# Three token-mixing branches emitted in steps between weight pieces, and one broadcast matmul in two float32r parts

## The chip, the cores and the metric

The kernel runs on one core of a Trainium2 chip. The time is device microseconds of one execution; the number compared is the median of several runs, and a profile is one further execution with its own time. The engines are called as the profile calls them: PE (TensorE, with PEld for its weight loads), DVE (VectorE), ACT (ScalarE) and SP, whose queue issues the DMAs.

## The reference, cut to what matters

The network is two blocks on 256 tokens of 2048 channels, all in float32. The second block, which alone is touched, has two layers; each is a mixing stage and a feed-forward stage. A mixing stage projects the normalised input and feeds four branches, whose outputs (512 channels each) are joined by one output matrix:

```python
p = (u @ w_in[l]).astype(jnp.float32)
p_ret, p_hgrn, p_ml, p_rw = split_cols_2(p, GROUP_COLS)
o_ret = retention_group(p_ret)
o_hgrn = hgrn2_group(p_hgrn, lower_bounds[l], hgrn_norm_w[l])
o_ml = mlstm_group(p_ml, ...)
o_rw, v_first = rwkv7_group(p_rw, v_first, ...)
mixed = jnp.concatenate([o_ret, o_hgrn, o_ml, o_rw], axis=-1) @ w_out[l]
h = h + rms_norm_2(mixed, norm_post_mix[l])
```

Each branch has 8 heads of 64 channels and is a linear attention over the tokens with a decay of its own: fixed per head in retention, from a gate per channel in hgrn, from two gates per head in mlstm. In mlstm the scores of a head are `q k^T * exp(log_decay - m_t)`, where `m_t` is a running maximum over the tokens; the output is divided by `max(|sum of scores|, exp(-m_t))`.

## The kernel before

Every large product reads its weights once from memory, in pieces of 128 x 1024 values (512 KB, three buffers). A piece is split by `weights` (L208) into two float32r parts: ACT copies `whi`, DVE subtracts to get `wlo`; `mm3` (L220, its matmuls on L223) then makes three matmuls, high by high, high by low and low by high. In the projections of the mixing stage a piece is 24 matmuls of 256 columns, in the output matrix 12 of 512 columns. `by_channels`, `by_tokens1` and `group_block` walk over the pieces and after each piece call `next(self.side, None)`, which emits one step of a generator; only the rwkv branch is such a generator.

In each mixing stage (`mixing`, L1639) the order of emission is: rwkv's projections; mlstm's gates; mlstm for heads 0 to 3 and for heads 4 to 7 ("halves"); hgrn's first half; the part of the output matrix for mlstm; hgrn's second half; retention's first half; the output part for hgrn; retention's second half; what is left of rwkv; the output parts for rwkv and, last, for retention. Each half is four projections (16 pieces) and then its inner part, emitted in one go.

The inner parts, with the lines that the trace names:

- mlstm: `decays` makes an exponent per head in one PSUM bank: two bf16 matmuls (L1266) put in the causal mask, and L1268 adds the running maxima `MX` of the head to all 128 partitions. L1268 is a float32 matmul with 8 rows and 384 columns, which the trace lists as two records; there are four in a half, 16 in all. ACT takes the exponentials (L1271). Then `pair_scores` (L1092), a product on DVE (L1279), the head's output (`head_out`, L1099 to L1101, 64 columns each) and its denominator (L1283 to L1285, one column each); afterwards a normalisation.
- hgrn: eight levels, each with exponentials, two transposes, four scores (L1178), masks, four outputs (L1188).
- retention: four heads; a table of decays comes by DMA (L1070, issued by SP), the scores are multiplied by it on DVE (L1075), then `head_out`.

The stages' tiles come from pools by tag with a fixed number of buffers (`g2` 12, `a3` 2), and a scheduler orders the instructions of each engine: what was emitted earlier goes first when its inputs are ready by the scheduler's own estimate. The order is fixed in the program, and on the chip each engine keeps to it.

Of the kernel before, what the change touches and what calls it, by code (L numbers as in the profile page):

```python
# [114 lines left out]
SECOND = dict(r2=16, g2=12, r1=5, a3=2, vf=2, mx=1, lora=1, nmu=1, mid=4, st=1, rtab=2, gate=3, den=2)  # L115
# [24 lines left out]
class Emitter:  # L140
    def __init__(self, tc, st, a, gains):
# [6 lines left out]
        self.side = iter(())  # L148
# [76 lines left out]
    def by_tokens(self, xg, w, c0, n):  # L225
# [3 lines left out]
        for k in range(0, 16, j):  # L229
# [6 lines left out]
            next(self.side, None)  # L236
        return [o[:, :n] for o in out]

    def by_channels(self, xg, w, c0, n):
# [5 lines left out]
        for k in range(0, 16, j):  # L245
# [7 lines left out]
            next(self.side, None)  # L253
# [22 lines left out]
    def group_block(self, yg, w, k0, cb):  # L276

        ps = [self.bank("m") for _ in range(2)]
        for k in range(0, 4, 2):
# [5 lines left out]
            next(self.side, None)  # L285
# [733 lines left out]
    def by_tokens1(self, xg, w, c0, n):  # L1019
# [3 lines left out]
        for k in range(0, 16, j):  # L1023
# [7 lines left out]
            next(self.side, None)  # L1031
# [17 lines left out]
    def retention(self, hf, xg, w, rows, tabs, yg):  # L1049
# [15 lines left out]
        o = self.bank("o").rearrange("p (m c) -> p m c", m=2)  # L1065
        for h in range(4):
            if h % 2 == 0:
                dec = self.t([P, 2, T], "g2")
                h0 = 4 * hf + h
                nc.sync.dma_start(dec, self.a["decay"][:, h0 * T : h0 * T + 2 * T].rearrange("p (h t) -> p h t", h=2))  # L1070
            if h % 2 == 0:
                pss = self.pair_scores(qT, kT, h // 2)
            ps = pss[h % 2]
            a = self.t([P, 384], "a3")
            nc.vector.tensor_mul(a[:, :T], ps[:, :T], dec[:, h % 2])  # L1075
            nc.vector.tensor_mul(a[:, T:], ps[:, T : T + P], dec[:, h % 2, :P])
            self.head_out(o, a, h, v)
        of = o.rearrange("p m c -> p (m c)")
        f = self.head_scale(of, 8, 64)
        y = self.t([P, 512], "y")  # L1080
        y3 = y.rearrange("p (h d) -> p h d", h=8)
        nc.vector.tensor_mul(y3, of.rearrange("p (h d) -> p h d", h=8), f.unsqueeze(2).to_broadcast([P, 8, 64]))
        nc.vector.tensor_mul(y, y, sz.rearrange("p m c -> p (m c)"))
        self.turned_rows(lambda b: self.split([q[:, 2 * hf : 2 * hf + 2] for q in yg], b), y)
# [18 lines left out]
    def hgrn(self, l, hf, xg, w, yg):  # L1103
# [38 lines left out]
        dg = g2()  # L1142
        nc.vector.tensor_mul(dg, q, k)
        nc.vector.tensor_mul(dg, self.pair_sums(dg, 2)[0], v)
        o = self.bank("o").rearrange("p (a t) -> p a t", a=2)
        nc.tensor.matmul(o.rearrange("p a t -> p (a t)"), self.c("ident"), dg.rearrange("p a t -> p (a t)"),
                         start=True, stop=False, skip_group_check=True)
        for h in (128, 64, 32, 16, 8, 4, 2, 1):
            nb = T // (2 * h)
            cm = cum[128 if h >= 32 else 32]  # L1150

            hv = lambda x, i: x.rearrange("p a (b j k) -> p (a b) j k", j=2, k=h)[:, :, i]
            cp = lambda x: x.rearrange("p a (b k) -> p (a b) k", k=h)
            n = 2 * nb
            ex = self.t([P, 2, 2, P], "g2")
            eq, ek = ex[:, 0], ex[:, 1]
            mid = hv(cm, 0)[:, :, h - 1 : h].to_broadcast([P, n, h])
            if h == 128:
                nc.vector.tensor_copy(cp(eq), hv(cm, 1))
            else:  # L1160
                nc.vector.tensor_sub(cp(eq), hv(cm, 1), mid)
            nc.vector.tensor_sub(cp(ek), mid, hv(cm, 0))
            nc.scalar.activation(ex, ex, AF.Exp)
            nc.vector.tensor_mul(cp(eq), cp(eq), hv(q, 1))
            nc.vector.tensor_mul(cp(ek), cp(ek), hv(k, 0))

            vh = self.t([P, 384], "a3")[:, :T].rearrange("p (a c) -> p a c", a=2)
            nc.scalar.copy(cp(vh), hv(v, 0))
            b = self.bank()[:, :T].rearrange("p (a c) -> p a c", a=2)
            self.transposes([b[:, i] for i in range(2)], [vh[:, i] for i in range(2)])  # L1170
            vc = self.t([P, 384], "a3")[:, :T]
            nc.scalar.copy(vc, b.rearrange("p a c -> p (a c)"))
            am = self.t([P, 2, 2, P], "g2")
            pss = [self.bank()[:, :T].rearrange("p (a t) -> p a t", a=2) for _ in range(2)]
            for i in range(2):
                for par in range(2):
                    r = slice(64 * par, 64 * par + 64)
                    nc.tensor.matmul(pss[par][:, i], ek[r, i], eq[r, i], start=True, stop=True)  # L1178
            for par in range(2):
                if h == 128:  # L1180
                    nc.scalar.copy(am[:, par], pss[par])
                else:
                    nc.vector.tensor_mul(am[:, par], pss[par], self.c({1: "ident", 64: "pair"}.get(h, f"same{h}")).unsqueeze(1).to_broadcast([P, 2, P]))
# [455 lines left out]
    def mixing(self, l, X):  # L1639
# [20 lines left out]
        for hf in range(2):  # L1660
            self.mlstm(l, hf, xg, w, rows, gates, ys[2])
# [176 lines left out]
```

## Time and profile before

| | us |
|---|---|
| median of 3 runs (lowest, highest) | 3941.05 (3933.78, 3945.38) |
| profiled execution, its own time | 3934.05 |
| its span in the trace | 3932.2 |
| PE busy (matmuls) | 3843.8, 98% |
| DVE busy, ACT busy | 2376.1 (60%), 1806.8 (46%) |
| mean granted clock of PE | 0.983 |

Busy time of PE is that of pipelined matmuls, so a PE that is busy all the time may still work slowly. The granted clock tells how fast: 1.00 stands for 2.4 GHz, 0.50 for 1.2 GHz. The mixing stage of the first layer runs from about 1046 to 1704 us of the span, that of the second from about 2466 to 3170 us; each is followed by a feed-forward stage.

### The profile page before, as it was taken

How to read it: one execution, taken by the hardware profiler on the slowest of the kernel's cores; microseconds unless marked ns; L12 is line 12 of the kernel's file. 1: busy time of each engine (PE TensorE's matmuls, PEld its weight loads, DVE VectorE, ACT ScalarE, POOL GpSimd, SP SyncE). 2: the span in 40 equal slices, each digit the busy share in tenths (PEclk: the TensorE clock that was granted, in tenths of full speed). 3: DMA queues.
4: the chain of work that ended last, by engine and by line, in shares of the span. 5: the costliest groups of instructions: out<-in, count | busy, mean ns of one | idle time of the engine just before them, and what ended most of it. 6: DMA issues, size and time to landing. Idle time of an engine off the chain costs nothing.

```text
span 3932.2 us, 54691 instructions
## 1 busy us (share of the span) xinstructions
PE 3843.8 (98%) x21408; PEld 3220.0 (82%) x21408; DVE 2376.1 (60%) x4126; ACT 1806.8 (46%) x2455; POOL 0.2 (0%) x4
## 2 busy tenths in 40 slices
PE   9999999999999999999999999999999999999998
PEld 7878877788889988878888888888888878888886
DVE  6666677666665565664555556764666565555556
ACT  5545455554543554354443434543554354444433
POOL 0000000000000000000000000000000000000000
PEclk9999999999999999999999999998999999999999
DMA  7664544655643333566666666543334656666665
GB/s 237 193 175 129 165 142 144 177 161 166 198 120 108 108 107 116 170 188 187 186 183 187 183 187 192 152 119 97 92 113 123 188 172 187 183 187 185 186 185 166
DMA packets 402644, 633.64 MB, mean 161 GB/s; under 512 B 28081, under 2 KB 164017, under 8 KB 402385
## 3 DMA queue, kind: packets, MB, share of 16 engines
q1 hardware_dynamic: 399744, 624.70, 53.1%
q10 hardware_dynamic: 2640, 5.44, 0.4%
q8 instruction: 168, 2.75, 0.3%
q14 instruction: 92, 0.75, 0.1%
HBM read 623.77 MB, written 6.29 MB: 160 GB/s over the span
## 4 chain that ended last, share of the span: by engine, by line
PE 77%; DVE 5%; ACT 2%; DMA 2%; issue 1%; DVEq 0%; SPq 0%; ACTq 0%
PE b L223 66%; PE b L317 3%; DVE wlo L218 1%; PE b L1492 1%; PE b L1486 1%; ACT whi L217 1%; PE b L1188 1%; PE b L1092 1%; PE b L1178 1%; DMA g<-in_decay_dram 0%; PE b L1465 0%; PE b L471 0%; PE b L1268 0%; PE b L505 0%; DMA wraw<-in_w_ffn_down_dram 0%
## 5 line engine op out<-in xcount | busy, mean ns | idle before, releaser
L218 DVE TENSOR_TENSOR wlo<-wraw,whi 128x1024 fp32r<-128x1024 f32 x1144 | 1392.5, 1218 | 1080.7 <-ACT whi L217 1078.1
L217 ACT CAST whi<-wraw 128x1024 fp32r<-128x1024 f32 x1144 | 1195.9, 1046 | 1579.6 <-PE b L223 1462.2
L223 PE MATMUL b<-whi,xt 128*128 128x512 f32 (+1 forms) x5888 | 1694.3, 370 | 0.5 <-ACT g L1060 0.5
L223 PEld LDWEIGHTS b<-whi,xt 128*128 128x128 f32 x5888 | 1056.7, 189 | 194.2 <-issue 2.2
L223 PE MATMUL b<-wlo,xt 128*128 128x512 f32 (+1 forms) x2944 | 1083.2, 368 | 3.3 <-DVE wlo L218 3.1
L223 PE MATMUL b<-whi,yt 128*128 128x512 f32 x2304 | 745.1, 400 | 1.5 <-ACT yt L307 1.5
L223 PEld LDWEIGHTS b<-wlo,xt 128*128 128x128 f32 x2944 | 555.3, 189 | 101.9 <-DVE wlo L218 7.6
L223 PEld LDWEIGHTS b<-whi,yt 128*128 128x128 f32 x2304 | 432.6, 188 | 105.2 <-ACT yt L307 2.0
L223 PE MATMUL b<-xt,whi 128*128 128x256 f32 (+3 forms) x2688 | 516.5, 290 | 2.3 <-ACT xt L310 2.0
L223 PE MATMUL b<-wlo,yt 128*128 128x512 f32 x1152 | 459.0, 399 | 0.0
L223 PEld LDWEIGHTS b<-xt,whi 128*128 128x128 f32 (+3 forms) x2688 | 418.4, 189 | 19.2 <-issue 9.3
L223 PE MATMUL b<-xt,wlo 128*128 128x256 f32 (+3 forms) x1344 | 386.0, 287 | 0.0
L223 PEld LDWEIGHTS b<-wlo,yt 128*128 128x128 f32 x1152 | 217.2, 189 | 50.7 <-issue 0.6
L223 PEld LDWEIGHTS b<-xt,wlo 128*128 128x128 f32 (+3 forms) x1344 | 254.0, 189 | 3.9 <-issue 2.1
L223 PE MATMUL b<-whi,g 128*128 128x512 f32 (+1 forms) x384 | 108.1, 361 | 0.4 <-ACT g L307 0.4
L296 DVE TENSOR_TENSOR r<-b,r 128x512 f32<-128x512 f32 x144 | 92.2, 682 | 0.0
L223 PEld LDWEIGHTS b<-whi,g 128*128 128x128 f32 (+1 forms) x384 | 61.7, 162 | 14.3 <-ACT g L307 0.9
L317 PE MATMUL b<-gains,X 128*128 128x128 f32 x232 | 38.0, 300 | 32.6 <-DVE small L384 15.6
L223 PE MATMUL b<-wlo,g 128*128 128x512 f32 (+1 forms) x192 | 68.8, 358 | 0.0
L296 DVE TENSOR_TENSOR X<-b,X 128x512 f32<-128x512 f32 x96 | 62.7, 684 | 5.4 <-PE b L223 5.4
L317 PEld LDWEIGHTS b<-gains,X 128*128 128x128 f32 x232 | 29.9, 155 | 39.4 <-issue 26.0
L485 ACT ACTIVATE soft<-b,small,esmall 128x256 f32<-128x256 f32 (+1 forms) x88 | 44.9, 517 | 36.2 <-DVE small L482 32.6
(468 smaller groups left out, 2855.8 us busy)
## 6 DMA issues: line engine op xcount, KB each, us to landing
wraw<-in_w_in_dram SPq DMA_DIRECT2D x248, 512.0 KB, 3.7
wraw<-in_w_ffn_gate_dram SPq DMA_DIRECT2D x176, 512.0 KB, 3.7
wraw<-in_w_ffn_up_dram SPq DMA_DIRECT2D x176, 512.0 KB, 3.7
wraw<-in_w_ffn_down_dram SPq DMA_DIRECT2D x176, 512.0 KB, 3.7
wraw<-in_w_out_dram SPq DMA_DIRECT2D x128, 512.0 KB, 3.7
wraw<-in_even_w_in_dram SPq DMA_DIRECT2D x104, 512.0 KB, 3.6
wraw<-in_odd_w_in_dram SPq DMA_DIRECT2D x96, 512.0 KB, 3.7
wraw<-in_mem_w_kv_dram SPq DMA_DIRECT2D x32, 512.0 KB, 3.8
```

The costliest lines, as they stand in the source:

```text
L217: nc.scalar.copy(hi, raw)
L218: nc.vector.tensor_sub(lo, raw, hi.bitcast(FT))
L223: self.nc.tensor.matmul(out, l[x], r[y], start=start and i == 0, stop=stop and i == 2, **kw)
L296: self.nc.vector.tensor_add(dst[cb][m], ps[m], dst[cb][m])
L317: self.nc.tensor.transpose(o, s, self.c("ident")[:n, :n])
L485: nc.scalar.activation(pt[:, i], ps3[:, i], AF.Exp, scale=fs[:, i : i + 1], bias=nb[:, i : i + 1], accum_out=sm[:, i : i + 1])
L1092: self.nc.tensor.matmul(res[par][:, c], kT[r, i, ss], qT[r, i, ts], start=True, stop=True)
L1178: nc.tensor.matmul(pss[par][:, i], ek[r, i], eq[r, i], start=True, stop=True)
L1188: nc.tensor.matmul(out, vc[:, i * P + 64 * par : i * P + 64 * par + 64], am[:, par, i], start=False, stop=h == 1, skip_group_check=True)
L1486: mm(ps[:, i].rearrange("p (b k) -> p b k", k=h), gb[0][:, i], left(inv[:, i]), start=True, stop=True)
L1492: mm(ps[:, i], it[:, i], pl[:, i], start=True, stop=True)
```

## The change

The inner parts of mlstm, hgrn and retention become generators, which the three functions return after their projections. `mixing` puts them in a queue; after each weight piece `step` emits one step of rwkv and one step of the first generator in the queue. Before an output part that needs a branch, `end_of` emits what is left of it. A half of mlstm has 7 steps, one of hgrn 10, one of retention 3: 40 in a layer, 80 in all. So a half's inner part stands between the pieces of the next projection or output part. Within mlstm, the exponents of two heads are a step, and each head's product, output and denominator one more.

In `mlstm_gates` the running maxima are split into two float32r parts, by the same ACT copy and DVE subtraction as the weights, and L1268 becomes two float32r matmuls (L1298 of the changed kernel) that add both parts. What is computed stays the same.

```diff
+    def step(self):
+        next(self.side, None)
+        while self.queue:
+            try:
+                next(self.queue[0])
+                return
+            except StopIteration:
+                self.queue.pop(0)
+
+    def end_of(self, gen):
+        while any(q is gen for q in self.queue):
...
-            next(self.side, None)
+            self.step()
...
-        MX = self.t([P, 384], "mx")[:8]
-        nc.vector.tensor_tensor_scan(MX[:, :T], ai, ai, 0.0, OP.max, OP.max)
-        nc.vector.tensor_copy(MX[:, T:], MX[:, P:T])
-        nc.vector.tensor_add(x, F, MX[:, :T])
+        nc.vector.tensor_tensor_scan(M, ai, ai, 0.0, OP.max, OP.max)
+        MX = [self.t([P, 384], "mx", FR)[:8] for _ in range(2)]
+        for c, t in ((slice(0, T), slice(0, T)), (slice(T, 384), slice(P, T))):
+            self.split([q[:, c] for q in MX], M[:, t])
+        nc.vector.tensor_add(x, F, M)
...
-            sel = self.c("ident")[:8, hh : hh + 1].to_broadcast([8, P])
+                sel = self.identr[:, hh : hh + 1].to_broadcast([8, P])
...
-            nc.tensor.matmul(pd[:, :384], sel, MX, start=False, stop=True, skip_group_check=True)
+                for i, q in enumerate(MX):
+                    nc.tensor.matmul(pd[:, :384], sel, q, start=False, stop=i == 1, skip_group_check=True)
...
                     dms = [decays(h + x) for x in range(2)]
+                    yield
                     pss = self.pair_scores(qT, kT, h // 2)
...
                 nc.vector.tensor_copy(den[:, :, h], db)
+                yield
...
-        for hf in range(2):
-            self.mlstm(l, hf, xg, w, rows, gates, ys[2])
-        self.hgrn(l, 0, xg, w, ys[1])
+        ml = [queued(self.mlstm(l, hf, xg, w, rows, gates, ys[2])) for hf in range(2)]
+        hg = [queued(self.hgrn(l, 0, xg, w, ys[1]))]
...
+        self.end_of(ml[1])
         self.out_group(ys[2], wo, 2 * 512, acc, True)
-        self.hgrn(l, 1, xg, w, ys[1])
-        self.retention(0, xg, w, rows, tabs, ys[0])
+        hg.append(queued(self.hgrn(l, 1, xg, w, ys[1])))
+        rt = [queued(self.retention(0, xg, w, rows, tabs, ys[0]))]
+        self.end_of(hg[1])
         self.out_group(ys[1], wo, 512, acc, False)
-        self.retention(1, xg, w, rows, tabs, ys[0])
+        rt.append(queued(self.retention(1, xg, w, rows, tabs, ys[0])))
         for _ in self.side:
             pass
         self.out_group(ys[3], wo, 3 * 512, acc, False)
+        self.end_of(rt[1])
```

What this does to the order on PE is shown at three places. In the changed kernel the lines are shifted: L240 is L223 of before, L1114 is L1092, L1121 to L1123 are L1099 to L1101, L1295 and L1298 are L1266 and L1268, L1314 to L1316 are L1283 to L1285, L1088 is L1070. Names: `b` is a PSUM bank, `xt` the input, `whi` and `wlo` a weight piece, `g` queries, keys and values, `a` the decays times scores.

First place, PE, first half of mlstm in the first layer: from the scores of two heads to the second head's output, before the change.

```order
L1092 MATMUL b_11144<-g_10562,g_10733 128x256
L1092 MATMUL b_11144<-g_10562,g_10733 128x128
L223 MATMUL b_11200<-xt,whi 128x256 x2
L1099 MATMUL b_11091<-g_10899,a_11133 128x64
L1100 MATMUL b_11091<-g_10899,a_11133 128x64
L1101 MATMUL b_11091<-g_10899,a_11133 128x64
L1283 MATMUL b_11143<-consts_307,a_11133 128x1
L1284 MATMUL b_11143<-consts_307,a_11133 128x1
L1285 MATMUL b_11143<-consts_307,a_11133 128x1
L223 MATMUL b_11200<-xt,wlo 128x256
L1099 MATMUL b_11091<-g_10899,a_11140 128x64
L1100 MATMUL b_11091<-g_10899,a_11140 128x64
```

The same place of the changed kernel, around the first head of a pair; the pieces of L240 go on on both sides.

```order
L240 MATMUL b_11097<-xt,wlo 128x256
L240 MATMUL b_11097<-xt,whi 128x256 x2
L1121 MATMUL b_11144<-g_10905,a_11151 128x64
L1122 MATMUL b_11144<-g_10905,a_11151 128x64
L1123 MATMUL b_11144<-g_10905,a_11151 128x64
L1314 MATMUL b_11208<-consts_307,a_11151 128x1
L1315 MATMUL b_11208<-consts_307,a_11151 128x1
L1316 MATMUL b_11208<-consts_307,a_11151 128x1
L240 MATMUL b_11097<-xt,wlo 128x256
L240 MATMUL b_11097<-xt,whi 128x256 x2
L240 MATMUL b_11097<-xt,wlo 128x256
L240 MATMUL b_11097<-xt,whi 128x256 x2
```

Before, two weight matmuls stand ahead of the first head and one between it and the next. Now 11 weight matmuls precede the first head's six small ones and 13 follow them (the other 12 of each lie outside the rows shown); the next weight piece begins after the second head.

Second place, PE, the exponents of two heads in the same half, before.

```order
L223 MATMUL b_11200<-xt,whi 128x256
L1266 LDWEIGHTS identb_9137
L1266 MATMUL b_11129<-laterb,identb_9137 128x128
L1266 LDWEIGHTS identb_9137
L1266 MATMUL b_11129<-laterb,identb_9137 128x128
L1268 MATMUL b_11129<-mx,gains 128x384
L1266 LDWEIGHTS identb_9137
L1266 MATMUL b_11136<-laterb,identb_9137 128x128
L1266 LDWEIGHTS identb_9137
L1266 MATMUL b_11136<-laterb,identb_9137 128x128
L1268 MATMUL b_11136<-mx,gains 128x384
L223 MATMUL b_11200<-xt,whi 128x256
```

And in the changed kernel.

```order
L1520 MATMUL b_11300<-r_11253,r_11128 128x64 x4
L1295 LDWEIGHTS identb_9137
L1295 MATMUL b_11307<-laterb,identb_9137 128x128
L1295 LDWEIGHTS identb_9137
L1295 MATMUL b_11307<-laterb,identb_9137 128x128
L1298 MATMUL b_11307<-mx,identr 128x384 x2
L1295 LDWEIGHTS identb_9137
L1295 MATMUL b_11315<-laterb,identb_9137 128x128
L1295 LDWEIGHTS identb_9137
L1295 MATMUL b_11315<-laterb,identb_9137 128x128
L1298 MATMUL b_11315<-mx,identr 128x384 x2
L240 MATMUL b_11335<-xt,whi 128x256 x2
```

Each float32 matmul of L1268 has become two matmuls of 384 columns, and a whole weight piece now follows where the scores of L1092 followed one weight matmul.

Third place, SP and PE, the second half of retention in the second layer. SP before:

```order
L216 DMA wraw<-in_w_out_dram 128x2x512 x5
L1070 DMA g_27788<-in_decay_dram 128x512
L1070 DMA g_27808<-in_decay_dram 128x512
L216 DMA wraw<-in_w_out_dram 128x2x512 x3
L1602 DMA y<-in_norm_post_mix_dram 128x512
```

SP in the changed kernel, with the lines shifted as on PE (L233 is L216, L1636 is L1602).

```order
L233 DMA wraw<-in_w_out_dram 128x2x512 x5
L1088 DMA g_27834<-in_decay_dram 128x512
L1088 DMA g_27872<-in_decay_dram 128x512
L233 DMA wraw<-in_w_out_dram 128x2x512 x5
L1636 DMA y<-in_norm_post_mix_dram 128x512 x2
```

PE before: from the last weight matmuls ahead of the first head's output to the second pair's scores.

```order
L223 MATMUL b_27858<-whi,yt 128x512
L223 MATMUL b_27857<-whi,yt 128x512
L1099 MATMUL b_27787<-g_27660,a_27796 128x64
L1100 MATMUL b_27787<-g_27660,a_27796 128x64
L1101 MATMUL b_27787<-g_27660,a_27796 128x64
L1092 MATMUL b_27810<-g_27387,g_27524 128x256
L1099 MATMUL b_27787<-g_27660,a_27802 128x64
L1100 MATMUL b_27787<-g_27660,a_27802 128x64
L1101 MATMUL b_27787<-g_27660,a_27802 128x64
L1092 MATMUL b_27811<-g_27387,g_27524 128x256
L1092 MATMUL b_27810<-g_27387,g_27524 128x128
L1092 MATMUL b_27811<-g_27387,g_27524 128x128
```

And in the changed kernel.

```order
L240 MATMUL b_27813<-whi,yt 128x512
L1121 MATMUL b_27833<-g_27686,a_27842 128x64
L1122 MATMUL b_27833<-g_27686,a_27842 128x64
L1123 MATMUL b_27833<-g_27686,a_27842 128x64
L240 MATMUL b_27813<-wlo,yt 128x512
L1121 MATMUL b_27833<-g_27686,a_27848 128x64
L1122 MATMUL b_27833<-g_27686,a_27848 128x64
L1123 MATMUL b_27833<-g_27686,a_27848 128x64
L240 MATMUL b_27813<-whi,yt 128x512
L240 MATMUL b_27814<-whi,yt 128x512
L240 MATMUL b_27814<-wlo,yt 128x512
L240 MATMUL b_27814<-whi,yt 128x512
```

On SP the decays stand behind the same five pieces of the output matrix. On PE, 13 matmuls of 512 columns stood between the scores (just ahead of the rows shown) and the first head; now the scores come after the first 12 of them and 7 more follow. The second pair's scores, which stood among the first pair's outputs, now come after the rest of a piece.

## Rows read from the trace of the kernel before

**Rows 1.** The page: PE's busy time, and its clock in 40 slices.

```profile
PE 3843.8 (98%) x21408; PEld 3220.0 (82%) x21408; DVE 2376.1 (60%) x4126; ACT 1806.8 (46%) x2455; POOL 0.2 (0%) x4
...
PEclk9999999999999999999999999998999999999999
```

**Rows 2.** Stretches: start and end, length, each engine's busy time, clock, DMA.

```profile
core 0: us, PE busy (x) PEld busy (x) DVE busy (x) ACT busy (x) POOL busy (x), PEclk, DMA share, GB/s
1206.40:1212.90 6.50, 6.11 (x54) 5.46 (x52) 3.03 (x7) 2.27 (x4) 0.00 (x0) 1.00 0.28 74
1212.90:1229.90 17.00, 17.00 (x62) 13.38 (x61) 5.52 (x14) 2.30 (x6) 0.00 (x0) 0.50 0.11 35
1298.10:1315.20 17.10, 17.10 (x66) 13.54 (x65) 3.28 (x8) 2.69 (x7) 0.00 (x0) 0.50 0.21 61
2660.10:2677.20 17.10, 17.10 (x60) 13.18 (x60) 5.43 (x13) 2.30 (x6) 0.00 (x0) 0.50 0.16 48
2745.50:2769.20 23.70, 23.70 (x94) 19.87 (x94) 7.14 (x21) 4.19 (x10) 0.00 (x0) 0.50 0.24 67
3103.90:3114.30 10.40, 10.40 (x36) 8.47 (x36) 2.76 (x6) 0.60 (x1) 0.00 (x0) 0.51 0.16 56
1380.00:1480.00 100.00, 99.48 (x776) 85.28 (x775) 60.97 (x122) 53.11 (x82) 0.00 (x0) 1.00 0.39 111
```

**Rows 3.** The same view for the weight matmuls (L223) alone: PE, PEld, clock.

```profile
1206.40:1212.90 6.50, 0.50 (x3) 0.19 (x1) 1.00 0.28 74
1380.00:1480.00 100.00, 69.27 (x416) 54.95 (x417) 1.00 0.39 111
```

**Rows 4.** Timeline of PE at full clock: start, duration, engine, line, operation, tiles.

```profile
1199.22 0.40 PE L223 MATMUL b<-whi,xt 128*128 128x256 f32 x2
...
1199.58 0.40 PE L223 MATMUL b<-whi,xt 128*128 128x256 f32 x2
...
1201.33 0.91 PE L1268 MATMUL b<-mx,gains 8*128 8x384 f32 x2
1202.17 0.23 PE L1266 MATMUL b<-laterb,identb 128*128 128x128 bf16 x1
...
1210.38 0.43 PE L1099 MATMUL b<-g,a 128*128 128x64 f32 x2
...
1211.81 0.71 PE L1465 MATMUL b<-X 64*128 64x128 f32 x6
```

**Rows 5.** Timeline of PE at half clock, the same kinds of work.

```profile
1214.78 1.64 PE L1268 MATMUL b<-mx,gains 8*128 8x384 f32 x2
1216.36 0.58 PE L223 MATMUL b<-xt,whi 128*128 128x256 f32 x1
...
1223.90 0.52 PE L1099 MATMUL b<-g,a 128*128 128x64 f32 x2
...
1226.31 0.77 PE L223 MATMUL b<-xt,whi 128*128 128x256 f32 x2
...
1228.38 0.63 PE L223 MATMUL b<-xt,whi 128*128 128x256 f32 x2
...
1229.02 0.63 PE L223 MATMUL b<-xt,whi 128*128 128x256 f32 x2
```

**Rows 6.** Timeline of PE, second half of retention, second layer.

```profile
3099.51 0.63 PE L223 MATMUL b<-whi,yt 128*128 128x512 f32 x2
...
3100.21 0.63 PE L223 MATMUL b<-whi,yt 128*128 128x512 f32 x2
...
3100.91 0.63 PE L223 MATMUL b<-whi,yt 128*128 128x512 f32 x2
3103.02 0.43 PE L1099 MATMUL b<-g,a 128*128 128x64 f32 x2 [1.48 <-DVE a L1075]
```

**Rows 7.** Waits: who waited for whom, us in total, times, longest.

```profile
ACT a L1271 <- PE b L1268: 30.8, 8, 6.2
...
PE b L1099 <- DVE a L1075: 4.0, 4, 1.5
```

More of the change, by code (lines that the diff above doesn't have):

```diff
@@ L196, in small @@
         return self.t([P, 16], tag)[:, :n]
+    def step(self):
[8 more added lines that the diff above has]
+        while any(q is gen for q in self.queue):
+            try:
+                next(self.queue[0])
+            except StopIteration:
+                self.queue.pop(0)
     def beside(self, gen, **alias):
@@ L252, in by_channels @@
                              kt == 0 and b % 2 == 0, kt == 15, skip_group_check=True)
-            next(self.side, None)
+            self.step()
         return out
@@ L284, in group_block @@
                              [q[:, i] for q in wt], k + i == 0, k + i == 3)
-            next(self.side, None)
+            self.step()
         return ps
@@ L1030, in by_tokens1 @@
                              skip_group_check=True)
-            next(self.side, None)
+            self.step()
         return out
@@ L1078, in retention, with steps @@
[L1078 to L1084, printed above, removed]
+        def steps():
+            o = self.bank("o").rearrange("p (m c) -> p m c", m=2)
+            for h in range(4):
+                if h % 2 == 0:
+                    dec = self.t([P, 2, T], "g2")
+                    h0 = 4 * hf + h
+                    nc.sync.dma_start(dec, self.a["decay"][:, h0 * T : h0 * T + 2 * T].rearrange("p (h t) -> p h t", h=2))
+                if h % 2 == 0:
+                    pss = self.pair_scores(qT, kT, h // 2)
+                ps = pss[h % 2]
+                a = self.t([P, 384], "a3")
+                nc.vector.tensor_mul(a[:, :T], ps[:, :T], dec[:, h % 2])
+                nc.vector.tensor_mul(a[:, T:], ps[:, T : T + P], dec[:, h % 2, :P])
+                self.head_out(o, a, h, v)
+                if h % 2:
+                    yield
+            of = o.rearrange("p m c -> p (m c)")
+            f = self.head_scale(of, 8, 64)
+            y = self.t([P, 512], "y")
+            y3 = y.rearrange("p (h d) -> p h d", h=8)
+            nc.vector.tensor_mul(y3, of.rearrange("p (h d) -> p h d", h=8), f.unsqueeze(2).to_broadcast([P, 8, 64]))
+            nc.vector.tensor_mul(y, y, sz.rearrange("p m c -> p (m c)"))
+            self.turned_rows(lambda b: self.split([q[:, 2 * hf : 2 * hf + 2] for q in yg], b), y)
@@ L1086, in pair_scores @@
+        return steps()
     def pair_scores(self, qT, kT, i):
@@ L1140, in hgrn @@
             cum[n] = cm
[L1142 to L1174, printed above, removed]
-            for i in range(2):
[L1176 to L1183, printed above, removed]
-            for i in range(2):
-                for par in range(2):
-                    r = slice(64 * par, 64 * par + 64)
-                    out = o[r, i].rearrange("p (b j k) -> p b j k", j=2, k=h)[:, :, 1]
-                    nc.tensor.matmul(out, vc[:, i * P + 64 * par : i * P + 64 * par + 64], am[:, par, i],
-                                     start=False, stop=h == 1, skip_group_check=True)
@@ L1202, in mlstm_gates @@
+        return steps()
     def mlstm_gates(self, l, xg, w, rows):
@@ L1274, in mlstm @@
-        for h in range(4):
-            if h % 2 == 0:
-                dms = [decays(h + x) for x in range(2)]
-                pss = self.pair_scores(qT, kT, h // 2)
-            dm, ps = dms[h % 2], pss[h % 2]
-            nc.vector.scalar_tensor_tensor(dm, ps[:, :384], 0.125, dm, OP.mult, OP.mult)
-            self.head_out(o, dm, h, v)
-            one = self.c("ones")[:, :1]
-            db = ps[:, 384:386]
-            nc.tensor.matmul(db[:, 0:1], dm[:, :P], one, start=True, stop=True)
-            nc.tensor.matmul(db[:, 1:2], dm[:, P:T], one, start=True, stop=False)
-            nc.tensor.matmul(db[:, 1:2], dm[:, T:], one, start=False, stop=True)
-            nc.vector.tensor_copy(den[:, :, h], db)
@@ L1306, in shifted @@
+        return steps()
     def shifted(self, ps, dst, mu, one_mu):
```

161 lines of the change are left out of this document (108 added, 53 removed).

## The prediction, made before the result was known

> **What bounds the kernel now.** I read the page first: PE is busy for 98% of the span and every other engine for 60% or less [rows 1]. So time can come only from making PE's work shorter or faster, and its few idle moments are worth little. The clock line then shows 9 everywhere but in one slice [rows 1]; a mean of 0.983 leaves 1.7% of the clock's pulses, so I asked the view of stretches for the granted clock over the two mixing stages, a few us at a time. In each it stands at 1.00 except at the stage's joints with the feed-forward stages and rwkv's start, which the change leaves alone, and in five stretches of 17.0, 17.1, 17.1, 23.7 and 10.4 us at 0.50, that is 1.2 GHz [rows 2]. The first four are the four halves of mlstm's inner part, the fifth is the second half of retention in the second layer. Within them PE is busy all the time [rows 2]: it does not wait, it works at half speed.
>
> What did PE do before the clock fell? In the 6.5 us ahead of the first fall it was busy for 6.11 us, but with weight matmuls for only 0.50 us [rows 2, 3]; the rest were small ones: scores of 64 rows, heads of 64 columns, denominators of one column. In hgrn's inner part, which the scheduler already mixes with weight pieces, the weight matmuls are 69.27 of 99.48 us and the clock is 1.00 [rows 2, 3]. That contrast is the base of my forecast.
>
> **The change part by part.** All sums are made against the profiled execution, 3934.05 us, 1.85 us more than its span; the median of the three runs lies 7.0 us above it.
>
> *The steps of mlstm and retention, and the clock.* Now every step is followed by a weight piece: 24 matmuls at 0.12 us each (three in 0.36 us from 1199.22 to 1199.58) make 2.9 us [rows 4]. The steps between take about 2 us by my estimate (two heads' masks and maxima, or scores with one head's six matmuls, which alone are 1.43 us from 1210.38 to 1211.81, plus rwkv's own step) [rows 4]. So weight matmuls would be over half of PE's time here, nearer to hgrn's 70% than to the 8% ahead of the fall. I take it that the clock then stays at 1.00 in all five stretches. What that gives: three weight matmuls take 0.64 us at half clock against 0.36 (0.56 of it), a head's six 2.41 against 1.43 (0.59), the float32 broadcast 1.58 against 0.84 (0.53) [rows 4, 5]. With 0.57 for the mixture, 43% of 85.3 us go: 36.7 us. With the extremes of the three ratios it is 34.7 to 39.9 us; if the clock falls as often as before, it is 0.
>
> *The broadcast of the maxima.* A float32 matmul of L1268 takes 0.84 us at full clock (1201.33 to 1202.17) [rows 4]. No row has a float32r matmul of 384 columns and 8 rows. The weight matmuls, float32r too, take 0.12 us for 256 columns [rows 4] and 0.233 for 512 (three in 0.70 us) [rows 6], so I estimate 0.175 for 384, and 0.35 for the two. Sixteen times 0.49 us saved is 7.8 us. The bound on the other side is that each part costs as much as the float32 matmul did: 16 x 0.84 = 13.4 us more. I take the saving, because the operand type that sets the weight matmuls' pace is the one used here. The split of the maxima itself (two more copies on ACT and two subtractions on DVE in each layer, less one DVE copy, on 8 partitions) lies in the gates, with 16 projection pieces of 2.9 us to come before the first use: 0, and were that cover gone, a few times 0.5 us in each layer.
>
> *hgrn's steps.* Its levels were mixed with pieces before and PE idles for only 0.5 us of 100 there [rows 2]. Fixing one level to one piece can win at most those 0.5 us and I cost it at 0; what it could lose is the third rival.
>
> *Moved waits.* In retention the first product waits for the decays' DMA, and PE for the product: 4.0 us in four halves, 1.5 us at the longest [rows 7]. On SP the two decays keep their place behind five pieces of the output matrix. On PE the scores of the shown half move behind 12 matmuls of 0.233 us, and 7 instead of 13 follow, so the first head is reached 6 x 0.233 = 1.4 us later and its wait of 1.48 us [rows 6] is all but used up. Queued behind the waiting head are the weight matmuls of the output part, as before. In mlstm ACT's exponentials wait for the broadcast, as they do now (30.8 us over 8 waits) [rows 7]; behind them on ACT stand the copies of the next weight pieces, and three buffers of a piece, 2.9 us each, cover PE meanwhile. DVE's product stands between scores and head in the same way; where only one weight matmul fills that gap, PE may wait some 0.4 us more. For eight pairs of heads that is 3 us, less 2 for retention: 1 us lost. The bounds are 3 us gained (all but 1 of retention's 4.0) and 8 lost (1.0 us, retention's mean wait, for each of the eight pairs).
>
> *Sum.* 3934.05 - 36.7 - 7.8 + 1 = 3890.6. The runs of before spread over 11.6 us, about one and a half of the slow stretches (7.3 us apiece), so I suspect that another run has another number of them; what else lifts the median stays. Of the 7.0 us between profile and median I keep 4. That gives 3895 us.
>
> **The rivals.**
>
> *Some of the stretches stay slow.* The steps keep runs of small matmuls: the longest in the changed order on PE is rwkv's four, four scores, four transposes, one weight matmul and one head's six, which by 1.43 us for the six I put between 3 and 4 us. In favour: the fifth fall came soon after weight matmuls that had run without a gap up to 3101.5, with 1.48 us of idle and one head between [rows 2, 6]. Against: before the first fall small work ran for 6 us nearly unbroken [rows 2, 3]. Two or three stretches back cost 15 to 22 us: 3910 to 3917.
>
> *Idle time alone decides the clock, or something else that the change leaves.* Then the stretches persist and only the broadcast is cheaper: 3934.05 - 7.8 + 4 = 3930, up to 3933 with the whole distance to the median. For it speaks the 1.48 us of idle ahead of the fifth fall [rows 6]; against it that PE idled only 0.39 us in the 6.5 ahead of the first and not at all in the 17 that followed [rows 2]. The Trainium skill, "TensorE: Matmul & The Clock Gate", section "HAM oscillation — how this bites in real kernels", tells of the clock falling when PE waits for a DMA, and gives the rule to avoid idle gaps. By that rule a busy PE would keep its clock and mixing in weight pieces would change nothing, which is the time just given; the first four stretches contradict it, the fifth agrees, and so this rival's chance is small.
>
> *The broadcast gains nothing.* If 8-row float32r parts cost as much as the float32 matmul each, the sum is 3934.05 - 36.7 + 13.4 + 1 + 4 = 3916.
>
> *The steps stall PE, and the kernel is slower.* 80 steps now sit in the in-order queues of ACT and DVE ahead of the casts and subtractions of the next weight piece. Should PE run dry once in each step, as it does at retention's first head (1.0 us a time) [rows 7], that is 80 us against 44.5 saved: 3934.05 - 44.5 + 80 + 4 = 3974. It decides from 0.56 us a step. Against it: hgrn's 32 levels already work in this way at 0.5 us of PE idle in 100 [rows 2], with DVE busy 61% and ACT 53% there.
>
> **How the numbers follow.** The forecast, 61%: 3882 to 3905. Some stretches stay, 19%: 3910 to 3917. The broadcast gains nothing, 6%: 3916. Idle alone, 8%: 3930 to 3933. Stalls, 6%: above 3941. Against the median, 0.3% is 11.8 us, about what runs of this kernel can tell from no change. The first three cases are faster than 3929.2: 86%. Idle alone falls within 0.3%: 8%; stalls are slower: 6%. The range 3880 to 3920 takes in the first three cases, with some 5% of them outside.
>
> **What would show it.** Right: the granted clock at 1.00 through mlstm and retention in both layers; two records of the broadcast about 0.175 us apart; the first mixing stage about 18 us shorter (43% of 34.1, and 3.9 for eight broadcasts) and the second about 26 (43% of 51.2, and 3.9); PE idle no larger than before. Wrong: stretches at 0.50 in the inner parts; records of the broadcast 0.4 us or more apart; idle ahead of weight matmuls released by `whi` or `wlo`. The forecast fails if the clock answers to something other than the share of weight matmuls in PE's work.

## The result, and the profile after

The changed kernel takes 3895.11 us in the median of four runs (3892.5 to 3899.5), the kernel before 3941.85 us beside it; the ratio is 0.9889 with a 95% interval from 0.9874 to 0.9903, so it is faster by 1.1%. The prediction was 3895 us. That it fits so well is partly luck: several terms were mis-sized and their errors cancel, and what follows is mostly about one of them, hgrn's steps. The profiled execution took 3899.5 us (span 3897.7).

The page of the changed kernel, PE's busy time and its clock in 40 slices, to set beside [rows 1]:

```profile
PE 3811.6 (98%) x21408; PEld 3195.3 (82%) x21408; DVE 2377.3 (61%) x4129; ACT 1808.8 (46%) x2459; POOL 0.2 (0%) x4
...
PEclk9999999999999999999999999999999999999999
```

As many matmul records as before take 32.2 us less of PE, and the slice with an 8 is gone. The stretches of the changed kernel that answer to [rows 2] (start and end, length, busy time of each engine, granted clock): the two halves of mlstm in the first layer, the two in the second, the end of retention in the second layer, and hgrn:

```profile
1210.00:1240.00 30.00, 29.17 (x251) 26.61 (x248) 18.20 (x35) 12.99 (x20) 0.00 (x0) 1.00 0.32 95
1302.00:1332.00 30.00, 28.76 (x218) 26.22 (x217) 20.89 (x47) 26.06 (x38) 0.00 (x0) 1.00 0.36 110
2644.00:2674.00 30.00, 29.17 (x250) 26.61 (x247) 18.06 (x35) 13.00 (x20) 0.00 (x0) 1.00 0.32 97
2736.00:2766.00 30.00, 28.76 (x220) 26.43 (x219) 21.80 (x49) 26.22 (x38) 0.00 (x0) 1.00 0.31 95
3108.00:3118.00 10.00, 9.21 (x40) 6.97 (x39) 7.21 (x9) 5.79 (x10) 0.00 (x0) 1.00 0.87 273
1380.00:1480.00 100.00, 97.89 (x759) 85.63 (x757) 55.19 (x111) 48.78 (x72) 0.00 (x0) 1.00 0.35 106
```

All of these are at 1.00, the five that were at half clock among them. The view of the weight matmuls alone, in the first of them and in hgrn, answers to [rows 3]:

```profile
1210.00:1240.00 30.00, 15.91 (x120) 14.55 (x120) 1.00 0.32 95
...
1380.00:1480.00 100.00, 67.46 (x437) 55.54 (x435) 1.00 0.35 106
```

In mlstm weight matmuls are now 53% of the time, against 0.50 of 6.50 us ahead of the fall before. To see what the change is worth as a whole, take each mixing stage from mlstm's gates to its end, first and second layer; before:

```profile
1135.77:1704.54 568.77, 551.51 (x4068) 493.01 (x4066) 341.81 (x689) 263.07 (x380) 0.00 (x0) 0.97 0.43 129
2583.44:3162.65 579.21, 560.71 (x4068) 500.32 (x4066) 343.46 (x693) 263.17 (x380) 0.00 (x0) 0.95 0.43 126
```

and after:

```profile
1139.47:1695.21 555.74, 540.40 (x4068) 485.21 (x4066) 342.10 (x690) 264.04 (x382) 0.00 (x0) 0.99 0.42 132
2574.84:3128.68 553.84, 538.68 (x4068) 483.69 (x4066) 343.45 (x694) 264.08 (x382) 0.00 (x0) 1.00 0.42 132
```

The two stages are 13.0 and 25.4 us shorter, 38.4 together: 33.1 less busy time of PE and 5.3 less idle. (The span fell by 34.5, since the work ahead of the first stage, which the change leaves alone, happened to take 3.7 us more.)

PE's waits in these stages after the change (us in total, times, longest), for [rows 7]:

```profile
PE b L334 <- DVE r L1607: 3.4, 2, 1.7
PE b L240 <- DVE wlo L235: 3.0, 4, 1.1
...
PE b L1121 <- DVE a L1310: 1.7, 2, 0.8
...
PE b L1121 <- DVE a L1093: 0.6, 2, 0.4
```

Retention's wait has fallen from 4.0 to 0.6 us. mlstm's heads wait once a layer for 0.8 (0.4 before), and weight pieces are late by 3.0 us in all, where the same view of the kernel before has no such wait.

Last, the groups of hgrn's inner part in the first stage (busy time, mean ns of one): the transposes, the scores of a level (64 rows), its output matmuls (64 columns). Before:

```profile
L1188 PE MATMUL b<-g,a 128*64 128x128 f32 x128 | 16.4, 291 | 0.0
...
L1178 PE MATMUL b<-g 64*128 64x128 f32 x128 | 11.4, 297 | 0.3 <-DVE g L1165 0.3
...
L317 PE MATMUL b<-gains,a 128*128 128x128 f32 x32 | 9.1, 315 | 0.0
```

and after:

```profile
L1202 PE MATMUL b<-g 64*128 64x128 f32 x128 | 19.6, 298 | 0.3 <-DVE g L1189 0.2
...
L1212 PE MATMUL b<-g,a 128*64 128x128 f32 x128 | 16.5, 291 | 0.0
...
L334 PE MATMUL b<-gains,a 128*128 128x128 f32 x32 | 7.0, 290 | 0.0
```

The scores' 128 records (a float32 matmul here is listed as two) are as long as before, one by one, but cover 8.2 us more; the transposes win 2.1. The second stages show the same, so in both layers this is 12.2 us that the change lost, and the prediction had put hgrn's steps at 0.

### The profile page after: what moved, and what is told of

It reads as the page before. It is cut to its first block, busy times and chain, and to the rows that moved or that the text cites. A ratio compares the mean times of both kernels' runs of the same rounds, so it can differ in the third digit from the quotient of the medians.

```text
span 3897.7 us, 54665 instructions
## 1 busy us (share of the span) xinstructions
PE 3811.6 (98%) x21408; PEld 3195.3 (82%) x21408; DVE 2377.3 (61%) x4129; ACT 1808.8 (46%) x2459; POOL 0.2 (0%) x4
## 4 chain that ended last, share of the span: by engine, by line
PE 78%; DVE 4%; ACT 2%; DMA 1%; issue 1%; DVEq 0%; SPq 0%; ACTq 0%
PE b L240 67%; PE b L334 3%; DVE wlo L235 1%; ACT whi L234 1%; PE b L1202 1%; PE b L1520 1%; PE b L1526 1%; PE b L1212 1%; DMA wraw<-in_w_out_dram 1%; PE b L488 0%; PE b L522 0%; PE b L1499 0%; PE b L1032 0%; DVE k L1005 0%; DMA wraw<-in_w_ffn_gate_dram 0%
## 5 line engine op out<-in xcount | busy, mean ns | idle before, releaser
L240 PE MATMUL b<-whi,xt 128*128 128x512 f32 (+1 forms) x5888 | 1695.1, 370 | 0.9 <-ACT whi L234 0.9
L240 PEld LDWEIGHTS b<-whi,xt 128*128 128x128 f32 x5888 | 1056.8, 188 | 197.9 <-issue 5.6
L240 PE MATMUL b<-wlo,xt 128*128 128x512 f32 (+1 forms) x2944 | 1084.1, 368 | 4.2 <-DVE wlo L235 4.0
L240 PE MATMUL b<-whi,yt 128*128 128x512 f32 x2304 | 744.6, 399 | 1.5 <-ACT yt L324 1.5
L240 PEld LDWEIGHTS b<-wlo,xt 128*128 128x128 f32 x2944 | 555.1, 189 | 102.9 <-DVE wlo L235 8.6
L240 PEld LDWEIGHTS b<-whi,yt 128*128 128x128 f32 x2304 | 431.1, 188 | 107.5 <-issue 3.0
L240 PE MATMUL b<-xt,whi 128*128 128x256 f32 (+3 forms) x2688 | 508.2, 287 | 2.3 <-ACT xt L327 2.0
L240 PE MATMUL b<-wlo,yt 128*128 128x512 f32 x1152 | 458.0, 398 | 0.0
L240 PEld LDWEIGHTS b<-xt,whi 128*128 128x128 f32 (+3 forms) x2688 | 411.2, 186 | 14.8 <-issue 3.8
L240 PE MATMUL b<-xt,wlo 128*128 128x256 f32 (+3 forms) x1344 | 381.8, 284 | 2.3 <-DVE wlo L235 2.3
L240 PEld LDWEIGHTS b<-wlo,yt 128*128 128x128 f32 x1152 | 216.6, 188 | 50.4 <-issue 1.4
L240 PEld LDWEIGHTS b<-xt,wlo 128*128 128x128 f32 (+3 forms) x1344 | 250.2, 186 | 6.4 <-DVE wlo L235 2.7
L240 PE MATMUL b<-whi,g 128*128 128x512 f32 (+1 forms) x384 | 108.1, 361 | 0.4 <-ACT g L324 0.4
L240 PEld LDWEIGHTS b<-whi,g 128*128 128x128 f32 (+1 forms) x384 | 61.7, 162 | 14.4 <-ACT g L324 0.9
L240 PE MATMUL b<-wlo,g 128*128 128x512 f32 (+1 forms) x192 | 68.9, 359 | 0.4 <-DVE wlo L235 0.4
```

Source lines behind the costliest of these rows:

```text
L240: self.nc.tensor.matmul(out, l[x], r[y], start=start and i == 0, stop=stop and i == 2, **kw)
```

## The experiments

Medians of the kernel before, beside these runs, are 3939.36 us for the first four, 3942.26 for the next four and 3939.35 for the last two; each ratio is to its own. "Low time" is the sum of the time at the lower granted clock, read from the view of stretches in pieces of half a us between 1040 and 3200 us, which holds both mixing stages (a piece with both clocks counts in proportion): 126.3 us before, 47.8 after. It belongs to one profiled execution, and executions differ: the granted clock of the kernel before is 0.978 to 0.984 in the runs beside these, and 0.983 in its profile.

**1. The steps alone.** All three parts in steps, the maxima broadcast in float32 as before:

```diff
...
-for i, q in enumerate(MX):
-    nc.tensor.matmul(pd[:, :384], sel, q, start=False, stop=i == 1, skip_group_check=True)
+nc.tensor.matmul(pd[:, :384], sel, MX, start=False, stop=True, skip_group_check=True)
...
```

> The changed kernel with the broadcast of the maxima as the one float32 matmul of before; the steps stay. My theory (the steps keep the clock up, the broadcast is a separate saving of 16 x 0.49 us): the clock at 1.00 through mlstm, about 3903 us against 3942 before, so 39 us faster and 8 us slower than the changed kernel. Rival (the float32 broadcast with its 8 rows is what brings the clock down): stretches at 0.50 come back in mlstm, 3925 us or more.

Measured: 3906.11 us, ratio 0.9906 (0.9891 to 0.9921), low time 41.7. The theory holds: the steps alone raise the clock. The timeline of PE in this kernel (start, us) shows a float32 broadcast of 0.84 us to the next start,

```profile
1210.89 0.91 PE L1296 MATMUL b<-mx,gains 8*128 8x384 f32 x2
1211.73 0.28 PE L1294 MATMUL b<-laterb,identb 128*128 128x128 bf16 x2
```

and in the changed kernel the two parts together take 0.54:

```profile
1210.98 0.61 PE L1298 MATMUL b<-mx,identr 8*128 8x384 f32 x2
1211.52 0.28 PE L1295 MATMUL b<-laterb,identb 128*128 128x128 bf16 x2
```

So a part takes 0.27 us on average, not the estimated 0.175, and 16 broadcasts win 4.8 us at full clock. In the two stages of the profiles PE is busy 6.0 us less in the changed kernel than here (1079.08 against 1085.10); the medians are 11.0 us apart, the ratios 0.0017, with intervals that overlap.

**2. The broadcast alone.** The kernel before with the two float32r parts and nothing in steps:

```diff
...
-nc.tensor.matmul(pd[:, :384], sel, MX, start=False, stop=True, skip_group_check=True)
+for i, q in enumerate(MX):
+    nc.tensor.matmul(pd[:, :384], sel, q, start=False, stop=i == 1, skip_group_check=True)
...
```

> The kernel before with the broadcast in two float32r parts alone; no steps. My theory: the four stretches of mlstm at 0.50 stay; 16 x 0.49 us or a little more (those at half clock save 0.88 each) is won, so about 3931 us against 3942. Rival (the broadcast brings the clock down): the stretches go and the time is 3905 us or less.

Measured: 3924.18 us, ratio 0.9958 (0.9946 to 0.9971), low time 119.5. The stretches stay, as the theory has it. The saving, 11 to 21 us by the interval, is larger than the 8 expected. Part of it is that some of the float32 matmuls lay at the lower clock, where one costs 1.58 us [rows 5]; but in the two stages of the profiles PE is busy only 7.3 us less than before, and idle 3.7 less. Where the rest comes from the runs don't show.

**3. mlstm's steps alone.** The change, with hgrn and retention emitted at once (a helper runs their steps to the end before the next piece):

```diff
-hg = [queued(self.hgrn(l, 0, xg, w, ys[1]))]
+hg = [at_once(self.hgrn(l, 0, xg, w, ys[1]))]
...
-rt = [queued(self.retention(0, xg, w, rows, tabs, ys[0]))]
+rt = [at_once(self.retention(0, xg, w, rows, tabs, ys[0]))]
...
```

> The changed kernel, but hgrn and retention are emitted in one go as before; only mlstm goes in steps. My theory: mlstm holds four of the five slow stretches, so nearly all of the gain is here; one stretch in retention may come back (4.5 us): about 3898 us against 3942. Rival (hgrn's steps win or lose several us by themselves): 3908 us or more, or 3888 or less.

Measured: 3889.95 us, ratio 0.9871 (0.9857 to 0.9885), low time 54.6. With less of the change the kernel is no slower but, by the medians, 5 us faster (the intervals of the ratios overlap). That lies between the theory's 3898 and the rival's 3888, so the rival is right in part.

**4. Filler.** The kernel before, and 128 matmuls of 512 columns in mlstm's inner parts, whose results are overwritten:

```diff
+    def fill(self, bank, xg, n=4):
+        hi = xg[0][0]
+        for _ in range(n):
+            self.nc.tensor.matmul(bank, hi[:, 0, :P], hi[:, 0:2].rearrange("p a t -> p (a t)"), start=True, stop=True)
...
 res = [self.bank() for _ in range(2)]
+if xg is not None:
+    for b in res:
+        self.fill(b, xg)
...
 pd = self.bank()
...
+self.fill(pd, xg)
...
```

> The kernel before, without the change, with 128 matmuls of 512 float32r columns added whose result is thrown away: four into each PSUM bank of mlstm's exponents and scores, ahead of the real work. They are 128 x 0.233 = 29.8 us of PE time at full clock. My theory (the clock falls because PE's work here is nearly all small matmuls, and dense ones hold it up): the four stretches of mlstm vanish or shrink, 74.9 us x 0.43 = 32 us come back, and the kernel with more work takes no longer: 3930 to 3950 us. Rival (the order of the steps, or waits, made the gain; the clock does not answer to added matmuls): 30 us more at full clock, up to 60 at half: 3972 us or more.

Measured: 3937.45 us, ratio 0.9996 (0.9983 to 1.0009), low time 92.2. At 0.233 us each [rows 6] the filler is 29.8 us of PE's work, and the median did not move: the first of mlstm's four low stretches is gone and the others last about 10.5 us each, though two others have come, at 1577 and 3038 us. The granted clock of its 11 runs is 0.985 to 0.993, above all 15 of the kernel before beside them (0.979 to 0.984). In mlstm, idle time was not what held the clock down (PE was busy throughout the stretches [rows 2]); thin work, matmuls of few rows or columns, was.

**5. hgrn at once, retention in steps:**

```diff
-hg = [queued(self.hgrn(l, 0, xg, w, ys[1]))]
+hg = [at_once(self.hgrn(l, 0, xg, w, ys[1]))]
...
```

> The changed kernel with hgrn's inner part emitted at once, as before the change; retention and mlstm go in steps. Theory (the steps of hgrn alone are what the whole change loses against mlstm's steps alone): the four score matmuls of each level stand alternating between their two banks again, so that their line takes about 11.4 us in a layer's stretch against 19.6, and the time is that of mlstm's steps alone or a little less, 3886 to 3892. Rival (retention's steps lose too, or hgrn's lose nothing): 3895 or more.

Measured: 3881.15 us, ratio 0.9847 (0.9826 to 0.9868), below that of the changed kernel with no overlap. The scores' line takes 11.4 us again. hgrn's steps cost the change 14 us, 12.6 of them in the two stages of the profiles. By the medians retention's steps win 9 (from 3889.95 of experiment 3), more than the theory gave them, but the stages of the two profiles differ by only 1.1 us; the granted clock of the runs is 0.992 to 0.993 here and 0.990 to 0.992 there.

**6. The scores ahead of the transposes.** Everything in steps, one block moved in hgrn's level:

```diff
+am = self.t([P, 2, 2, P], "g2")
+pss = [self.bank()[:, :T].rearrange("p (a t) -> p a t", a=2) for _ in range(2)]
+for i in range(2):
+    for par in range(2):
+        r = slice(64 * par, 64 * par + 64)
+        nc.tensor.matmul(pss[par][:, i], ek[r, i], eq[r, i], start=True, stop=True)
 vh = self.t([P, 384], "a3")[:, :T].rearrange("p (a c) -> p a c", a=2)
...
 nc.scalar.copy(vc, b.rearrange("p a c -> p (a c)"))
-am = self.t([P, 2, 2, P], "g2")
-pss = [self.bank()[:, :T].rearrange("p (a t) -> p a t", a=2) for _ in range(2)]
...
-        nc.tensor.matmul(pss[par][:, i], ek[r, i], eq[r, i], start=True, stop=True)
```

> The whole change, all three parts in steps, but in each of hgrn's levels the scores are emitted ahead of the two transposes, so that both of the scores' banks are free when their turn comes and the four matmuls stand together, alternating between the banks, in 28 of 32 levels. Theory (the split scores are the loss): the scores' line falls from 19.6 to about 12 us in a layer's stretch, and the time from 3895 to 3878 to 3886, the fastest so far. Rival (the loss of hgrn's steps lies in waits or in the many switches between small and large matmuls, not in the scores' order): 3892 or more.

Measured: 3869.66 us, ratio 0.9816 (0.9794 to 0.9837): the fastest of all, 25 us ahead of the changed kernel. Its groups:

```profile
L1196 PE MATMUL b<-g 64*128 64x128 f32 x128 | 12.4, 299 | 0.0
...
L1212 PE MATMUL b<-g,a 128*64 128x128 f32 x128 | 10.5, 285 | 0.2
...
L334 PE MATMUL b<-gains,a 128*128 128x128 f32 x32 | 6.6, 287 | 0.0
```

The scores win back 7.2 us a layer, as the theory said. What it did not foresee is that the output matmuls fall too, from 16.5 to 10.5. The timeline of PE shows why. In the changed kernel a weight matmul mostly divides the four output matmuls of a level into one and three, and a level's scores fall into two pairs, with weight matmuls between them, because two banks take turns and the second pair's is still held by the transposes' result (x4 is two matmuls):

```profile
1373.23 0.43 PE L1212 MATMUL b<-g,a 128*64 128x128 f32 x2
1373.59 0.49 PE L240 MATMUL b<-whi,yt 128*128 128x512 f32 x1
1374.02 0.65 PE L1212 MATMUL b<-g,a 128*64 128x128 f32 x6
1374.60 0.50 PE L240 MATMUL b<-wlo,yt 128*128 128x512 f32 x1
...
1377.71 0.71 PE L1202 MATMUL b<-g 64*128 64x128 f32 x4
1378.35 0.50 PE L240 MATMUL b<-whi,yt 128*128 128x512 f32 x1
1378.69 0.40 PE L240 MATMUL b<-wlo,yt 128*128 128x512 f32 x1
1379.02 0.71 PE L1202 MATMUL b<-g 64*128 64x128 f32 x4
1379.65 0.73 PE L240 MATMUL b<-whi,yt 128*128 128x512 f32 x2
```

One output matmul holds PE for 0.36 us and three for 0.58; each pair of scores holds it for 0.64 or 0.63 us (1377.71 to 1378.35, 1379.02 to 1379.65). In experiment 6 all four stand together, and so do the four output matmuls:

```profile
1372.22 0.72 PE L1196 MATMUL b<-g 64*128 64x128 f32 x8
1372.86 0.50 PE L240 MATMUL b<-whi,yt 128*128 128x512 f32 x1
...
1375.61 0.66 PE L1212 MATMUL b<-g,a 128*64 128x128 f32 x8
1376.20 0.50 PE L240 MATMUL b<-wlo,yt 128*128 128x512 f32 x1
```

Four scores then hold PE for the same 0.64 us, and four output matmuls for 0.59. In experiment 3 (hgrn at once) a transpose divides the output matmuls:

```profile
1375.72 0.43 PE L1212 MATMUL b<-g,a 128*64 128x128 f32 x2
1376.09 0.33 PE L334 MATMUL b<-gains,a 128*128 128x128 f32 x1
1376.34 0.65 PE L1212 MATMUL b<-g,a 128*64 128x128 f32 x6
1376.93 0.33 PE L334 MATMUL b<-gains,a 128*128 128x128 f32 x1
```

There one holds it for 0.37 us and three for 0.59, as long as four that stand together. And a pair of scores alone costs as much as two pairs that stand together.

The Trainium skill, "TensorEngine Tiling (Array Packing)", section "Key Properties", has a rule of this kind: tiles of the array work in parallel, but a change of the tiling mode drains TensorE. The trace agrees in direction: the pairs use different halves of the array, and each return to full-size matmuls ends what could overlap. That a drain is the cause no run here shows by itself.

**7. The scores bank by bank, nothing between.** Experiment 3 with the two loops exchanged:

```diff
-for i in range(2):
-    for par in range(2):
+for par in range(2):
+    for i in range(2):
         r = slice(64 * par, 64 * par + 64)
         nc.tensor.matmul(pss[par][:, i], ek[r, i], eq[r, i], start=True, stop=True)
```

> Mlstm's steps alone (hgrn and retention at once), but hgrn's four score matmuls of a level are emitted bank by bank, two on the upper 64 rows and then two on the lower 64, with nothing between the pairs. Theory (two row halves overlap only when their matmuls alternate): a level's scores take about 1.3 us instead of 0.7, 32 levels make 10 to 19 us, and the time is 3900 to 3909 against the 3890 of the same kernel with alternating scores. Rival (it was the weight matmuls between the pairs that cost, not the order of the halves): 3888 to 3893.

Measured: 3899.85 us, ratio 0.9892 (0.9872 to 0.9913). The time lies at the lower edge of the theory's range, but the line that it rests on is not:

```profile
L1212 PE MATMUL b<-g,a 128*64 128x128 f32 x128 | 17.3, 292 | 0.7
...
L1202 PE MATMUL b<-g 64*128 64x128 f32 x128 | 11.6, 297 | 0.1
...
L334 PE MATMUL b<-gains,a 128*128 128x128 f32 x32 | 8.0, 306 | 0.0
```

The scores take 11.6 us, not 19: that the halves must alternate has fallen, and the rival is right that what stands between the pairs costs, though not in the time that it gave. In the two stages PE is busy 9.0 us longer than in experiment 3 and idle 5.4 longer (low time 58.0 against 54.6); where these come from stays open.

**8. mlstm at once.** The change, with mlstm's halves emitted whole:

```diff
-ml = [queued(self.mlstm(l, hf, xg, w, rows, gates, ys[2])) for hf in range(2)]
+ml = [at_once(self.mlstm(l, hf, xg, w, rows, gates, ys[2])) for hf in range(2)]
```

> The whole change, but with mlstm's inner parts emitted at once; hgrn and retention go in steps and the broadcast keeps its two float32r parts. Theory (mlstm's steps end the four low stretches of the clock, hgrn's steps lose some 6 us a layer): at least 55 us of the mlstm halves stay at the lower granted clock, and the time is 3920 to 3935. Rival (steps anywhere in the stage are enough for the clock, because mlstm's stretches hang on what follows them): under 25 us stay low there, and the time is 3905 or less.

Measured: 3935.09 us, ratio 0.9979 (0.9967 to 0.9992), low time 105.8. Its stretches in the first and second halves of mlstm, first layer:

```profile
1212.00:1229.00 17.00, 17.00 (x78) 14.97 (x79) 5.49 (x12) 2.45 (x6) 0.00 (x0) 0.51 0.22 62
1301.00:1315.00 14.00, 14.00 (x70) 13.66 (x70) 6.26 (x29) 2.73 (x6) 0.00 (x0) 0.51 0.14 40
```

The falls are back, with PE busy all the time; hgrn's and retention's steps alone don't end them. The clock's gain belongs to mlstm's own steps.

**9. hgrn at once, scores first.** Experiment 5 with the block of experiment 6 moved.

> Mlstm and retention in steps, hgrn at once, and hgrn's scores emitted ahead of the two transposes. Theory (hgrn's steps by themselves gain nothing; what counts is that the four scores and the four output matmuls of a level each stand together): the scores' line takes 11.4 us in a layer's stretch and the output line falls from 16.4 to about 10.5, with 2.5 us off the transposes, so 8.4 us a layer against the same kernel with the transposes first (3881), and the time is 3860 to 3869. Rival (hgrn's steps gain once its matmuls stand together, by covering its waits): 3874 or more, slower than the whole change with the scores first (3870).

Measured: 3876.33 us (3872.5 to 3881.25), ratio 0.9841 (0.9824 to 0.9857). The three groups are as the theory said (11.4, 10.5, 6.5 us), yet the time is the rival's. Its two stages:

```profile
1137.92:1685.61 547.69, 527.11 (x4068) 476.80 (x4066) 342.11 (x690) 263.56 (x382) 0.00 (x0) 0.99 0.45 134
2564.97:3109.48 544.51, 525.37 (x4068) 475.85 (x4066) 343.64 (x693) 263.40 (x382) 0.00 (x0) 0.99 0.45 134
```

and those of experiment 6:

```profile
1136.36:1674.68 538.32, 524.63 (x4068) 476.12 (x4066) 341.20 (x690) 264.11 (x382) 0.00 (x0) 1.00 0.46 137
2552.69:3092.30 539.61, 524.31 (x4068) 476.12 (x4066) 342.48 (x693) 263.75 (x382) 0.00 (x0) 1.00 0.45 135
```

PE's idle time is 39.7 us here and 29.0 in experiment 6. With a level's matmuls together, hgrn's steps do win, 7 us by the medians (the intervals of the ratios overlap, the runs themselves do not), by covering waits. How much is not exact: the profile here is of the longest of its runs, 4.9 us above the median, that of experiment 6 of the shortest, 6.4 below.

**10. The scores first, and nothing else.** The kernel before with that block moved.

> The kernel before, nothing in steps and the broadcast in float32, with one edit: hgrn's scores are emitted ahead of the two transposes. Theory (the order inside a level is worth the same without any steps): the output line falls from 16.4 to about 10.5 us a layer and the transposes from 9.1 to 6.6, 8.4 us a layer, and the time is 3921 to 3930; the low stretches of the clock stay. Rival (what the order saves in busy time comes back as waits or lower clock, because hgrn's chain is longer): 3935 or more.

Measured: 3936.59 us, ratio 0.9987 (0.9972 to 1.0002), low time 163.8. The groups fall here as well (11.4, 10.5 and 6.5 us), 8.5 us a layer, and of these 17 us the median shows 2.8; the interval runs from 11 us won to 0.8 lost. In the profile the low time is 37.5 us longer than before and PE's idle time in the two stages 42.0 us against 35.8. But this profile lies 8.1 us above its kernel's median and that of the kernel before 7.0 below its own, so the two overstate the fall: over all runs the mean granted clock is 0.980 here and 0.981 for the 17 runs beside. The time is the rival's; how much of the saving went to the clock and how much to waits stays open. The same edit that wins 25 us on the changed kernel wins nothing measurable on the old one.

## Why the prediction came out right, and which steps of it failed

- **The clock: right.** 85.3 us of low stretches were to vanish, and all five did; experiments 1, 3 and 8 show that steps do it, mlstm's above all. What it gave can be taken from the stages: PE is busy 33.1 us less although hgrn lost 12.2; less the broadcast's 4.8, that leaves 40.5 us, against 36.7 predicted with bounds of 34.7 and 39.9. A part of the 40.5 is in lines that merely lie better, which the runs don't separate. The low time gives less: it fell by 78.5 us, since stretches outside the five grew or came (one of 4 us at 1151), and at 43% that is 34 us by my estimate. That retention's steps end the fifth stretch is not shown: it is absent in experiment 3 too, where retention is emitted at once, and there the clock is 0.51 for 7.00 us in retention of the first layer (from 1632.5).
- **Idle time as the clock's rule: refuted for mlstm.** Its rival gave 3930 to 3933. The rule of the Trainium skill, "TensorE: Matmul & The Clock Gate", section "HAM oscillation — how this bites in real kernels", that idle gaps lower the clock, does not cover experiment 8, where PE is busy for 17.00 of 17.00 us at 0.51, nor experiment 4, where more work in the same places raised the clock.
- **The broadcast: right sign, wrong size.** Two parts take 0.54 us and not 0.35, so the term is 4.8 us and not 7.8 once the clock is up. Pace by column, carried over from the weight matmuls, does not hold for these matmuls of 8 rows; why, no run shows.
- **hgrn's steps at 0: wrong.** The step that failed reads "Fixing one level to one piece can win at most those 0.5 us and I cost it at 0; what it could lose is the third rival." (The stall that it calls the third rival stands fourth.) I looked at idle time alone, for gain and for loss. The loss lies in busy time: the weights that a step lets in between a level's pairs cost 8.2 us a layer in the scores, less 2.1 in the transposes. Experiment 5 prices the steps at 14 us, and experiment 6, which keeps them and puts a level's matmuls together, has the scores' 7.2 us back. The rival that I named, steps that stall PE, is not it: PE's idle time fell by 5.3 us.
- **Moved waits: the ones named come out near the 1 us lost.** Retention's wait shrank by 3.4 us and mlstm's heads pay 0.8 a layer, 0.4 more than before. I had called idle released by `wlo` a sign against me; there are 3.0 us of it, none before. PE's idle time is 30.5 us in the two stages, 35.8 before, so "no larger" holds; its fall of 5.3 us is more than the 3 that I had as the bound, since waits that I had not summed went too (for `tok` at L451 1.7 us a layer, for hgrn's `g` at L1143 1.3).
- **The total: right partly by cancellation.** From profile to profile I had 43.5 us, and it was 34.5: the 12.2 of hgrn, the 3.0 of the broadcast and 3.7 ahead of the first stage, against gains in the clock and the waits. That I kept 4 us of the distance from the profile to the median offset it: the changed kernel's profiled execution lies 4.4 us above its median, not 4 below. The stages, foretold 18 and 26 us shorter, are 13.0 and 25.4.

## What to carry to other kernels

Before you cut a block into steps, look at which of its small matmuls overlap on the array, and keep those together: give them banks that are free at the same moment, or emit them ahead of what holds the bank. Ask a step's price in busy time as well as in idle time. And where TensorE is busy throughout but its granted clock is low, dense matmuls that have to be done anyway are worth mixing into the thin ones, since they keep the clock up; the version with both (3869.66 us) is 1.8% faster than the kernel before.

## What the runs showed of the hardware

- 128 added matmuls of 512 columns, 29.8 us of work, cost no measurable time (ratio 0.9996, interval 0.9983 to 1.0009), with a granted clock of 0.985 to 0.993 in its runs against 0.979 to 0.984 without them.
- The lower clock does not need idle time: with mlstm's inner parts in one go it was 0.51 for 17.00 us in which PE was busy for all 17.00 (experiment 8), and with the same parts in steps the low time was 47.8 us in place of 105.8.
- Saving 17 us of PE's busy time by the groups' rows (8.5 us in each of two layers, experiment 10) shortened the median by only 2.8 us (interval: 11 us won to 0.8 lost).
- Two score matmuls of 64 rows hold PE for 0.64 us when weight matmuls stand on both sides, and four hold it for 0.64 us too, whether the halves alternate or not (11.4 and 11.6 us a layer).
- Two float32r matmuls of 8 rows and 384 columns hold PE for 0.54 us, a float32 one of the same shape for 0.84.
